# DeltaNet decays stacked at four partition offsets, two heads' state as one block-diagonal tile, and inverse products that alternate row groups

## The chip, the cores and the metric

The kernel runs on one NeuronCore of a Trainium2 chip. The metric is the device time of one execution in microseconds, from the first to the last instruction with what lies around them. Each kernel is run several times; the median counts.

## The reference, cut to what matters

The program is a network of two layers on 272 tokens (16 meta tokens and 256 of the input), width 1024. Each layer is an FFN, a mixer and another FFN. The mixer has four branches (two attentions, the gated DeltaNet and an RG-LRU); their outputs are gated and added. The DeltaNet branch, with `q`, `k` normalised and four heads of 64, works in chunks of 128 tokens:

```
g = -exp(a_log) * softplus(p_a + dt_bias);  beta = sigmoid(p_b)
G = cumsum(g) inside a chunk;  decay[i,j] = exp(G[i] - G[j]) for i >= j
m = I + strictly_lower(beta * (k k^T) * decay);   solve m for w, u
qk = lower((q k^T) * decay)
per chunk:  v_new = u - w S;  o = (q exp(G)) S + qk v_new
            S = S * exp(G_last) + (k exp(G_last - G))^T v_new
```

Everything is float32.

## The kernel before, in words

Activations stand transposed, features on partitions, tokens as columns. A product with a weight matrix is `wtile` (L437): a weight tile of 128x128 is split into a rounded part `wh` (ScalarE, L408) and a rest `wl` (VectorE, L410), and three fp32r matmuls add `wh`·`xh`, `wh`·`xl`, `wl`·`xh` into a PSUM tile `j` (`o`, `br`, `wo` in other places). These are called weight matmuls below. Weights come by DMA into `wf` and are split in pieces of 1024 columns, five pieces ahead at most.

The order on all engines is set when the program is built. Every branch is a Python generator (a chain); `poll` (L277) looks at each of them after a weight tile, and lets a chain issue its next step when a running estimate of the engines' clocks says that its input is there. Chain steps on TensorE are only looked at every third tile (`EVERY`), so nine weight matmuls stand between most of them. `mm` (L229) and `pe_go` (L211) hold the estimate of a matmul's cost; a tile of under 128 rows or columns is priced as if it ran alone. All engines take their instructions in the order so made.

The DeltaNet branch is two chains. `fab` (L1675) makes the decays. Twelve partitions, 96 to 107, hold the forget gate, the decay and beta of four heads; `gc` is the cumulated decay, `eg`, `be`, `eh` are exponentials. Twelve small transposes (L1731, tile `ns`), each of 12 partitions, bring four of these rows for three token tiles to token order, two selector products (`sel2`) add the last columns, and VectorE copies them to the SBUF tile `ns` and negates two parts of it. Then for each head a selector product on 12 partitions spreads `gc` over the rows (`dc`), three bf16 matmuls add the causal mask, one for each token tile, and ScalarE takes the exponential into `dec`. `nsv` (L1778) reads columns of `ns`.

`gdn` (L1878) and its helper chains do the rest. `g_qk` makes k·q (`kq`) and `gdn` k·k (`kk`), for each token tile and each half `e` of the partitions (two heads lie on partitions 0 to 63 and 64 to 127 of two tiles) two products into one PSUM tile. The matrix is then inverted in blocks of 16, by a VectorE loop of fifteen rounds (L1936), and combined to 32, 64 and 128 by products called p0, x0, p1, x1 (32x32 tiles, in four row groups of 32 partitions) and p2, x2 (64x64). In the profile their tiles are `p` and `x`. Last, for each token tile: k·S (`ks`) and q·S (`qs`), for each half two products of 64 rows into their own PSUM tile, `vn`, and the update `su` of the state `S`, which holds head pairs on two partition halves.

Of the kernel before, what the change touches and what calls it, by code (L numbers as in the profile page):

```python
# [71 lines left out]
class Prog:  # L72
# [471 lines left out]
    def setup2(self, c):  # L544
# [16 lines left out]
        self.maskk = self.const([P, P], BF16, "maskk")  # L561
# [14 lines left out]
        self.V(c, "tensor_copy", out=self.maskk, in_=mg)  # L576
# [5 lines left out]
        q = slice(96, 108)  # L582
# [3 lines left out]
        self.POOL(c, "affine_select", out=sel[q], in_=o4[q], pattern=[[-1, 4], [0, P]], compare_op=ALU.is_equal,  # L586
                                fill=0.0, base=-4, channel_multiplier=1)
# [17 lines left out]
        for x, dst in ((0, self.eye16), (1, self.st16)):  # L605
# [7 lines left out]
        self.POOL(c, "affine_select", out=misc[q, 512:768].rearrange("p (h c) -> p h c", h=4),  # L613
                                in_=self.ones[:, 0:1].to_broadcast([P, 256]).rearrange("p (h c) -> p h c", h=4)[q],
                                pattern=[[-1, 4], [0, 64]], compare_op=ALU.is_equal,
                                fill=0.0, base=-4, channel_multiplier=1)
# [1058 lines left out]
    def fab(self, c):  # L1675
# [26 lines left out]
        for a, n in TOK:  # L1702
            yield "dve"
            self.V(c, "tensor_tensor_scan", out=gc[q, a:a + n], data0=self.ones[q, 0:1].to_broadcast([12, n]), data1=lg[q, a:a + n],
                   initial=0.0, op0=ALU.mult, op1=ALU.add)
# [8 lines left out]
        eg, be = e, lg  # L1714
        for a, n in TOK:
            yield "dve"
            self.V(c, "tensor_scalar", out=eh[q, a:a + n], in0=gc[q, a:a + n], scalar1=gc[q, a + n - 1:a + n],
                   scalar2=-1.0, op0=ALU.subtract, op1=ALU.mult)
        yield AF.Exp
        self.A(c, eg[q, :T], gc[q, :T], AF.Exp)  # L1720
        yield AF.Exp
        self.A(c, be[q, :T], lg[q, :T], AF.Exp)
        yield AF.Exp
        self.A(c, eh[q, :T], eh[q, :T], AF.Exp)
        yield
        ps = yield from self.take_wait(c, "px", name="ns")
        for ti, (a, n) in enumerate(TOK):
            for x, src in enumerate((be, gc, eg, eh)):
                o = ti * 48 + x * 12
                yield "pe"  # L1730
                nc.tensor.transpose(ps[:n, o:o + 12], src[q, a:a + n], self.ident[q, 96:108])  # L1731
                self.pe_go(c, 13.0, 1, 107.0, 90.0)
        for pr in range(2):
            yield "pe"
            self.mm(c, ps[:, 160 + 3 * pr:163 + 3 * pr], self.sel2[q, pr, :],
                    eg[q, 15:T:128])
        yield
        ns = yield from self.take_wait(c, "S", name="ns")
        for ti, m in ((0, 16), (1, P), (2, P)):
            yield "dve"  # L1740
            self.V(c, "tensor_copy", out=ns[:m, ti * 48:ti * 48 + 48], in_=ps[:m, ti * 48:ti * 48 + 48])
        yield "dve"
        self.V(c, "tensor_copy", out=ns[:, 160:166], in_=ps[:, 160:166])
        self.give(ps, c.t)
        for ti, m in ((0, 16), (1, P), (2, P)):
            b = ti * 48

            yield "dve"
            self.V(c, "tensor_scalar", out=ns[:m, b:b + 4], in0=ns[:m, b + 8:b + 12], scalar1=-1.0, scalar2=None,
                   op0=ALU.mult)  # L1750
            yield "dve"
            self.V(c, "tensor_scalar", out=ns[:m, b + 12:b + 16], in0=ns[:m, b + 16:b + 20], scalar1=-1.0,
                   scalar2=None, op0=ALU.mult)
        self.ns = ns
        self.ev["ns"] = c.t
        yield

        dec = yield from self.take_wait(c, "L", [P, 4, T], name="dec")
        for h in range(4):
            ps = yield from self.take_wait(c, "px", name="dc")  # L1760
            yield "pe"
            self.mm(c, ps[:, :T], self.sel[q, h, :], gc[q, :T], True, False)
            for ti, (a, n) in enumerate(TOK):
                yield "pe"
                self.mm(c, ps[:, a:a + n], self.identb, self.maskk[:, :n], False, ti == 2)
            yield
            for ti, (a, n) in enumerate(TOK):
                yield AF.Exp
                self.A(c, dec[:n, h, a:a + n], ps[:n, a:a + n], AF.Exp,
                       bias=ns[:n, ti * 48 + 12 + h:ti * 48 + 13 + h])  # L1770
            self.give(ps, c.t)
            yield
        for s in st:
            self.give(s, c.t)
# [3 lines left out]
    def nsv(self, x, ti, n, h0=0, hs=4, step=1):  # L1778

        b = ti * 48 + (0, 12, 28, 40, 8)[x]  # L1780
        return self.ns[:n, b + h0:b + h0 + (hs - 1) * step + 1:step]
# [41 lines left out]
    def g_qk(self, c):  # L1823
# [4 lines left out]
        for ti in (1, 2, 0):  # L1828
            if ti == 0 and self.l == L - 1:
                continue  # L1830
            a, n = TOK[ti]
            for e in range(2):
                ps = yield from self.take_wait(c, "px", name="kq")
                p0 = 64 * e
                v = ps[:, 0:256].rearrange("p (x i) -> p x i", x=2)
                yield "pe"
                for x in range(2):
                    self.mm(c, v[:n, x, :n], self.cvt[f"gk{x}"][p0:p0 + 64, a:a + n],
                            self.cvt[f"gq{x}"][p0:p0 + 64, a:a + n])
                qd = QT[:, (ti - 1) * 4 + e:(ti - 1) * 4 + e + 3:2, :] if ti else self.mt[:, 4 + e:4 + e + 3:2, :]  # L1840
                yield "dve"
                self.V(c, "tensor_tensor", out=qd, in0=v[:n, :, :n], in1=self.dec[:n, e::2, a:a + n], op=ALU.mult)
                self.give(ps, c.t)
# [34 lines left out]
    def gdn(self, c):  # L1878
# [20 lines left out]
        for ti in (1, 2, 0):  # L1899
            a, n = TOK[ti]  # L1900
            for e in range(2):
                ps = yield from self.take_wait(c, "px", name="kk")
                p0 = 64 * e
                v = ps[:, 0:256].rearrange("p (x i) -> p x i", x=2)
                yield "pe"
# [3 lines left out]
                for x in range(2):  # L1909
                    h = e + 2 * x  # L1910
                    yield "dve"
                    self.V(c, "scalar_tensor_tensor", out=AT[:, (ti - 1) * 4 + h, :] if ti else mt[:, h, :],
                           in0=v[:n, x, :n], scalar=self.nsv(0, ti, n, h, 1),
                           in1=dec[:n, h, a:a + n], op0=ALU.mult, op1=ALU.mult)
                self.give(ps, c.t)
# [50 lines left out]
        for s in sl:  # L1966
            for hc in range(8):
# [7 lines left out]
        for s in sl:  # L1975
            for hc in range(8):
# [29 lines left out]
        for b in (0, 2):  # L2006
            for hc in range(8):
# [9 lines left out]
        for b in (0, 2):  # L2017
            s, t_ = sl[b], sl[b + 1]
            for hc in range(8):
                self.mm(c, v[s, hc, :], P1[t_, hc, :], Xh[t_, hc, :])  # L2020
                if b == 0:
                    self.mm(c, v[t_, hc, :], Xh[t_, hc, :], P1[t_, hc, :])
# [38 lines left out]
        outs = []  # L2061
        for ti in range(3):
# [3 lines left out]
            if ti:  # L2066
                for e in range(2):
                    ps = yield from self.take_wait(c, "px", name="ks")
                    p0 = 64 * e
                    v = ps[:, :P].rearrange("p (x d) -> p x d", x=2)  # L2070
                    yield "pe"
                    for x in range(2):
                        self.mm(c, v[:n, x, :], kn[x][p0:p0 + 64, a:a + n], S[p0:p0 + 64, x, :])
                    tk = yield from self.take_wait(c, "S", [P, 2, 64], name="tk")
                    yield "dve"
                    self.V(c, "tensor_tensor", out=tk[:n], in0=v[:n],
                           in1=self.nsv(2, ti, n, e, 2, 2)[:, :, None].to_broadcast([n, 2, 64]), op=ALU.mult)
                    self.give(ps, c.t)
                    yield "dve"
                    self.V(c, "tensor_tensor", out=h4(r[:n])[:, e::2, :], in0=h4(r[:n])[:, e::2, :], in1=tk[:n],  # L2080
                           op=ALU.subtract)
                    self.give(tk, c.t)
# [11 lines left out]
            if ti < 2:  # L2094
                S2 = yield from self.take_wait(c, "S", [P, 2, 64], name="S")
                ps = yield from self.take_wait(c, "px", name="su")
                yield "pe"
                for h in range(4):
                    p0 = 64 * (h % 2)
                    self.mm(c, ps[p0:p0 + 64, (h // 2) * 64:(h // 2) * 64 + 64], kd[:n, h * 64:(h + 1) * 64],  # L2100
                            r[:n, h * 64:(h + 1) * 64])
                for x in range(2):
                    yield "dve"
# [139 lines left out]
```

## Time and profile before

| | |
|---|---|
| median of three runs | 1363.91 us (1363.6 to 1367.29) |
| the profiled execution | 1363.22 us, span 1361.5 us |
| TensorE busy, instructions | 1338.8 us (98%), 10615 matmul records |
| VectorE busy | 879.6 us (65%) |
| ScalarE busy | 732.0 us (54%) |
| mean granted TensorE clock | 0.991 |

A float32 matmul shows as two records in the profile, a transpose and an fp32r matmul as one. The duration of a record has the way through the array in it, so records overlap; what a matmul costs the engine is read from the start of one to the start of the next.

### The profile page before, as it was taken

What the parts mean: (1) busy time and instruction counts of PE and PEld (TensorE: products, weight loads), DVE (VectorE), ACT (ScalarE), POOL (GpSimd) and SP (SyncE); (2) the same over time, 40 slices, a digit from 0 to 9 for tenths busy, and PEclk for the clock granted to TensorE, in tenths of its full rate; (3) what the DMA queues carried; (4) which work ended last, traced back from release to release, by engine and by line L of the source; (5) the groups of instructions that cost most, each with busy time, mean ns of one, the idle gap of its engine ahead of it and who ended that gap; (6) DMA issues with size and microseconds to landing.
All of it is one profiled execution on the core that took longest, in us unless ns stands there. A gap on an engine that the chain in (4) does not pass through costs nothing.

```text
span 1361.5 us, 25871 instructions
## 1 busy us (share of the span) xinstructions
PE 1338.8 (98%) x10615; PEld 1290.5 (95%) x10615; DVE 879.6 (65%) x1526; ACT 732.0 (54%) x1196; POOL 208.5 (15%) x287
## 2 busy tenths in 40 slices
PE   8999999999999999999999999999999999999997
PEld 7999999888999999999999999998889999999986
DVE  6765556668566876655566555567794678766653
ACT  5465445886454554444444445459843645644442
POOL 3533000000002242110011110010000032211100
PEclk9999999999799999999999999999998999999999
DMA  6666565332225555555555555653322365555551
GB/s 220 191 195 199 164 175 164 108 125 74 79 78 167 190 177 186 186 173 174 180 161 180 184 164 167 173 163 125 125 78 65 113 200 193 192 186 186 200 196 53
DMA packets 210886, 214.62 MB, mean 158 GB/s; under 512 B 13292, under 2 KB 200016, under 8 KB 210768
## 3 DMA queue, kind: packets, MB, share of 16 engines
q1 hardware_dynamic: 208608, 210.68, 48.1%
q0 software_dynamic: 2128, 2.29, 0.6%
q8 instruction: 83, 1.36, 0.4%
q14 instruction: 35, 0.29, 0.1%
q10 hardware_dynamic: 32, 0.01, 0.0%
HBM read 211.90 MB, written 1.05 MB: 156 GB/s over the span
## 4 chain that ended last, share of the span: by engine, by line
PE 81%; DVE 10%; ACT 6%; issue 2%; POOL 0%; DMA 0%; SPq 0%; ACTq 0%; DVEq 0%; POOLq 0%
PE j L230 52%; PE o L230 15%; PE fo L230 4%; DVE wl L183 3%; PE br L230 3%; ACT wh L207 2%; ACT L202 2%; PE wo L230 1%; PE x L230 1%; ACT gt L207 1%; DVE xl L183 1%; DVE sm L183 1%; PE p L230 1%; DVE tp L1939 1%; ACT sq L207 1%
## 5 line engine op out<-in xcount | busy, mean ns | idle before, releaser
L230 PE MATMUL j<-xh,wh 128*128 128x272 f32 (+2 forms) x2224 | 651.3, 293 | 0.1
L230 PE MATMUL j<-xh,wl 128*128 128x272 f32 (+2 forms) x2224 | 638.1, 287 | 0.1
L230 PE MATMUL j<-xl,wh 128*128 128x272 f32 (+2 forms) x2224 | 637.5, 287 | 0.0
L183 DVE TENSOR_TENSOR wl<-wf,wh 128x1024 fp32r<-128x1024 f32 (+2 forms) x406 | 492.3, 1221 | 176.0 <-ACT wh L207 175.1
L207 ACT ACTIVATE wh<-wf 128x1024 fp32r<-128x1024 f32 (+2 forms) x406 | 407.0, 1031 | 103.3 <-PE o L230 72.7
L230 PEld LDWEIGHTS j<-xh,wh 128*128 128x128 f32 (+1 forms) x2224 | 420.0, 189 | 4.6 <-issue 1.0
L230 PEld LDWEIGHTS j<-xl,wh 128*128 128x128 f32 (+1 forms) x2224 | 420.8, 189 | 0.6
L230 PEld LDWEIGHTS j<-xh,wl 128*128 128x128 f32 (+1 forms) x2224 | 420.6, 189 | 0.8 <-DVE wl L183 0.8
L230 PE MATMUL o<-act,wh 128*128 128x272 f32 x1056 | 198.9, 288 | 0.0
L230 PEld LDWEIGHTS o<-act,wh 128*128 128x128 f32 x1056 | 165.8, 188 | 0.0
L230 PE MATMUL o<-act,wl 128*128 128x272 f32 x528 | 152.1, 288 | 0.0
L194 POOL TENSOR_TENSOR g<-g,R 128x272 f32<-128x272 f32 (+1 forms) x88 | 86.4, 984 | 378.1 <-ACT g L207 378.1
L207 ACT ACTIVATE act<-g 128x272 fp32r<-128x272 f32 (+1 forms) x88 | 37.6, 428 | 135.2 <-DVE g L183 135.2
L207 ACT ACTIVATE g<-g 128x272 f32<-128x272 f32 (+1 forms) x88 | 37.4, 428 | 120.2 <-DVE g L183 119.7
L230 PEld LDWEIGHTS o<-act,wl 128*128 128x128 f32 x528 | 99.5, 188 | 0.0
L183 DVE TENSOR_TENSOR g<-j,g 128x272 f32<-128x272 f32 (+1 forms) x88 | 38.2, 434 | 54.6 <-PE j L230 51.1
L194 POOL TENSOR_TENSOR sq<-sq,sq 128x272 f32<-128x272 f32 (+1 forms) x36 | 32.8, 910 | 257.4 <-ACT sq L207 243.9
L202 ACT ACT_TABLE_LOAD x51 | 65.4, 1283 | 1.7 <-PEq L2231 0.8
L194 POOL TENSOR_TENSOR gt<-gt,gt 128x272 f32<-128x272 f32 (+1 forms) x32 | 35.4, 1130 | 198.1 <-DVE gt L183 198.0
L207 ACT ACTIVATE gt<-gt,pv 128x272 f32<-128x272 f32 (+1 forms) x64 | 30.0, 510 | 64.7 <-DVE gt L183 64.6
L183 DVE TENSOR_TENSOR g<-j,R 128x272 f32<-128x272 f32 (+1 forms) x88 | 37.9, 433 | 34.4 <-PE j L230 34.1
L230 PE MATMUL fo<-wh,act 128*128 128x512 f32 x176 | 55.3, 395 | 0.0
(332 smaller groups left out, 1377.8 us busy)
## 6 DMA issues: line engine op xcount, KB each, us to landing
wf<-in_ffn_wi_dram SPq DMA_DIRECT2D x86, 1024.0 KB, 5.2
wf<-in_ffn_wo_dram SPq DMA_DIRECT2D x34, 1024.0 KB, 5.2
wf<-in_w_gate_dram SPq DMA_DIRECT2D x32, 1024.0 KB, 5.2
wf<-in_w_in_dram SPq DMA_DIRECT2D x16, 1024.0 KB, 5.2
wf<-in_ffn_wo_dram SPq DMA_DIRECT2D x12, 768.0 KB, 4.8
wf<-in_w_branch_dram SPq DMA_DIRECT2D x16, 512.0 KB, 3.5
wf<-in_w_out_dram SPq DMA_DIRECT2D x8, 1024.0 KB, 5.4
wf<-in_w_in_dram SPq DMA_DIRECT2D x4, 512.0 KB, 3.9
```

What stands on the lines that cost most here:

```text
L183: getattr(self.nc.vector, op_)(**kw)
L194: getattr(self.nc.gpsimd, op_)(**kw)
L202: self.nc.scalar.preload_act_table_set(SETS[ok[0]])
L207: self.nc.scalar.activation(out=out, in_=in_, func=func, **kw)
L230: self.nc.tensor.matmul(out, lhsT, rhs, start=start, stop=stop)
L1939: nc.vector.stream_shuffle(tf[:, k * 12:], xf[:, k * 12:], mask=[k] * 16 + [16 + k] * 16)
```

## The change

In `fab` the rows that were in four tiles are written into one tile `pk`, zeroed before, at partitions 0 (beta), 32 (cumulated decay), 64 (its exponential) and 96 (decay to the end of the chunk). Three transposes of the whole tile replace the twelve. The selector products take all 128 partitions of `pk`. One mask of 272 columns takes the place of three mask matmuls for each head. k·q, k·k and the products p0, x0, p1, x1 are written so that neighbouring matmuls use different row groups; for k·q and k·k the two halves write two PSUM tiles. The state of two heads becomes a block-diagonal 128x128 tile, zeroed by GpSimd, so that k·S, q·S and the update are two products of 128 rows and columns each.

```diff
-        for _ in range(6):
+        for _ in range(5):
-        zs, e, sp, lg, gc, eh = st
+        zs, e, sp, lg, pk = st
+        nc.gpsimd.memset(pk[:, :T], 0.0)
+        g, u, w = slice(32, 44), slice(64, 76), slice(0, 12)
...
+        for ti, (a, n) in enumerate(TOK):
+            self.tr(c, ps[:n, ti * P:(ti + 1) * P], pk[:, a:a + n])
+        for pr in range(2):
+            self.mm(c, ps[:, 384 + 3 * pr:387 + 3 * pr], self.sel2[:, pr, :], pk[:, 15:T:128])
...
-        for ti, (a, n) in enumerate(TOK):
-            for x, src in enumerate((be, gc, eg, eh)):
-                o = ti * 48 + x * 12
-                yield "pe"
-                nc.tensor.transpose(ps[:n, o:o + 12], src[q, a:a + n], self.ident[q, 96:108])
...
-            self.mm(c, ps[:, :T], self.sel[q, h, :], gc[q, :T], True, False)
-            for ti, (a, n) in enumerate(TOK):
-                yield "pe"
-                self.mm(c, ps[:, a:a + n], self.identb, self.maskk[:, :n], False, ti == 2)
+            self.mm(c, ps[:, :T], self.sel[:, h, :], pk[:, :T], True, False)
+            self.mm(c, ps[:, :T], self.identb, self.maskk, False, True)
...
             for e in range(2):
-                ps = yield from self.take_wait(c, "px", name="kk")
-                p0 = 64 * e
-                v = ps[:, 0:256].rearrange("p (x i) -> p x i", x=2)
-                yield "pe"
-                for x in range(2):
-                    kk = kn[x][p0:p0 + 64, a:a + n]
-                    self.mm(c, v[:n, x, :n], kk, kk)
+                p2.append((yield from self.take_wait(c, "px", name="kk")))
+            v = [ps[:, 0:256].rearrange("p (x i) -> p x i", x=2) for ps in p2]
+            yield "pe"
+            for h in range(4):
+                kk = kn[h // 2][64 * (h % 2):64 * (h % 2) + 64, a:a + n]
+                self.mm(c, v[h % 2][:n, h // 2, :n], kk, kk)
...
-        for s in sl:
-            for hc in range(8):
+        for hc in range(8):
+            for s in sl:
                 self.mm(c, v[s, hc, :], AT[s, hc, s], Tc[s, hc, :])
...
+        for _ in range(2):
+            x = yield from self.take_wait(c, "S", [P, 2, P], name="S")
+            nc.gpsimd.memset(x.ap, 0.0)
+            states.append(x)
...
-                for e in range(2):
-                    ps = yield from self.take_wait(c, "px", name="ks")
...
-                    for x in range(2):
-                        self.mm(c, v[:n, x, :], kn[x][p0:p0 + 64, a:a + n], S[p0:p0 + 64, x, :])
+                ps = yield from self.take_wait(c, "px", name="ks")
+                yield "pe"
+                for x in range(2):
+                    self.mm(c, ps[:n, x * P:(x + 1) * P], kn[x][:, a:a + n], S[:, x, :])
```

The order on TensorE changes in these places.

TensorE in layer 0, where the decay columns are transposed (`ns`), before:

```order
L1731 MATMUL ns_2856<-ident_111,fab_2667 128x12
L230 MATMUL j_2928<-xh_82,wh_2769 128x272
L230 MATMUL j_2928<-xl_90,wh_2769 128x272
L230 MATMUL j_2928<-xh_82,wl_2770 128x272
L230 MATMUL j_2928<-xh_83,wh_2769 128x272
L230 MATMUL j_2928<-xl_91,wh_2769 128x272
L230 MATMUL j_2928<-xh_83,wl_2770 128x272
L230 MATMUL j_2928<-xh_84,wh_2797 128x272
L230 MATMUL j_2928<-xl_92,wh_2797 128x272
L230 MATMUL j_2928<-xh_84,wl_2798 128x272
L1731 MATMUL ns_2856<-ident_111,fab_2664 128x12
```

The same place in the changed kernel, behind the products and transposes of two attentions (`qu`, `vt`):

```order
L230 MATMUL qu_2812<-misc_2642,wq_1277 128x272
L241 MATMUL vt_2817<-ident_111,fv_372_2754 128x128
L241 MATMUL vt_2817<-ident_111,fv_377_2796 128x128
L241 MATMUL ns_2838<-ident_111,fab_2669 16x128
L241 MATMUL ns_2838<-ident_111,fab_2669 128x128 x2
L230 MATMUL ns_2838<-fab_2669,sel_778 128x3 x2
L230 MATMUL j_2798<-xh_83,wh_2707 128x272
```

The three transposes and the two selector products stand in one piece; the twelve single transposes, with nine weight matmuls between two of them, are gone.

TensorE in layer 0 at the k·q and k·k products (`kq`, `kk`; `cv` are q and k), before:

```order
L230 MATMUL j_3569<-xh_82,wl_3407 128x272
L230 MATMUL kq_3579<-cv_2987,cv_2894 128x128
L230 MATMUL kq_3579<-cv_3039,cv_2945 128x128
L230 MATMUL kk_3585<-cv_2894 128x128
L230 MATMUL kk_3585<-cv_2945 128x128
L230 MATMUL sc_3600<-ka_2562,qa_2561 128x144
```

And now:

```order
L230 MATMUL j_3375<-xh_85,wl_3249 128x272
L230 MATMUL kk_3389<-cv_2903 128x128
L230 MATMUL kk_3390<-cv_2903 128x128
L230 MATMUL kk_3389<-cv_2961 128x128
L230 MATMUL kk_3390<-cv_2961 128x128
L241 MATMUL nat_3415<-ident_111,cv_2903 128x128
```

The four products of a token tile go alternately into two PSUM tiles, and the group stands 63 weight matmuls earlier in the program, ahead of most of the attention scores (`sc`).

TensorE in layer 0 at the last steps of the inverse, p2 here, before:

```order
L230 MATMUL j_4365<-xh_82,wl_3978 128x272
L230 MATMUL sc_4351<-kt_2805,qt_2804 128x16
L230 LDWEIGHTS identb_698
L230 MATMUL sc_4351<-maskq_711,identb_698 128x16
L230 MATMUL pv_4406<-vl_2906,lt_4398 128x256
L230 MATMUL p_657_4412<-T_644_4307,AT_2573 64x64 x8
L241 MATMUL pl_4439<-ident_111,mp_4349 128x128
L241 MATMUL ot_4442<-ident_111,oa_4422 128x128 x2
L230 MATMUL j_4365<-xh_83,wh_3977 128x272
```

And now, where p2 is followed by five narrow score products with their masks (two shown) and x2 before the next weight matmul:

```order
L230 MATMUL p_650_4373<-T_633_4247,AT_2575 64x64 x8
L230 MATMUL sc_4381<-kt_2807,qt_2806 128x16
L230 LDWEIGHTS identb_698
L230 MATMUL sc_4381<-maskq_711,identb_698 128x16
L230 MATMUL sc_4366<-ka_2564,qa_2563 128x16
...
L230 MATMUL x_655_4403<-XF_4206,P_654_4394 64x64 x8
L230 MATMUL sc_4366<-ka_2564,qa_2563 128x16
L230 LDWEIGHTS identb_698
L230 MATMUL sc_4366<-maskq_711,identb_698 128x16
L241 MATMUL pl_4425<-ident_111,mp_4379 128x128
L230 MATMUL j_4270<-xh_86,wh_4007 128x272
```

Nine weight matmuls that stood between p2 and x2 now stand before p2.

## Rows read from the trace of the kernel before

**Rows 1.** The page, part 1: busy us, share, instructions of each engine.

```profile
PE 1338.8 (98%) x10615; PEld 1290.5 (95%) x10615; DVE 879.6 (65%) x1526; ACT 732.0 (54%) x1196; POOL 208.5 (15%) x287
```

**Rows 2.** The chain that ended last (start us, us, what), first FFN.

```profile
54.72 93.95 PE j L230 x750
```

**Rows 3.** Stretches: length; busy PE, PEld, DVE, ACT, POOL; granted clock; DMA share, GB/s.

```profile
360.58:374.23 13.65, 13.54 (x111) 12.46 (x109) 5.32 (x12) 6.92 (x28) 0.00 (x0) 0.50 0.24 78
1022.77:1029.60 6.83, 6.83 (x80) 5.95 (x79) 1.29 (x4) 1.90 (x6) 0.29 (x1) 0.50 0.01 2
...
301.40:348.20 46.80, 45.14 (x349) 40.97 (x349) 41.38 (x143) 30.63 (x75) 4.18 (x8) 1.00 0.25 80
976.90:1003.00 26.10, 24.03 (x198) 21.86 (x196) 23.91 (x81) 16.44 (x45) 0.70 (x2) 1.00 0.25 82
```

**Rows 4.** Timeline (start us, us, engine, line), layer 0, two decay transposes.

```profile
245.94 0.23 PE L1731 MATMUL ns<-ident,fab 12*128 12x12 f32 x1
...
247.41 0.23 PE L1731 MATMUL ns<-ident,fab 12*128 12x12 f32 x1
```

**Rows 5.** Timeline, layer 0: a product of two accumulated matmuls, a decay selector.

```profile
224.24 1.08 PE L230 MATMUL nq<-sq,ones 128*128 128x272 f32 x4
...
225.28 0.29 PE L230 MATMUL j<-xl,wh 128*128 128x272 f32 x1
...
259.62 0.28 PE L230 MATMUL j<-xh,wl 128*128 128x272 f32 x1
259.83 0.72 PE L230 MATMUL dc<-fab,sel 12*128 12x272 f32 x2
...
260.71 0.29 PE L230 MATMUL j<-xl,wh 128*128 128x272 f32 x1
```

**Rows 6.** Timeline, layer 0: k·q and k·k, mixed and alone.

```profile
307.28 0.27 PE L230 MATMUL kk<-cv 64*128 64x128 f32 x1
307.29 0.27 PE L230 MATMUL kq<-cv,cv 64*128 64x128 f32 x1
307.39 0.27 PE L230 MATMUL kk<-cv 64*128 64x128 f32 x1
...
309.72 0.71 PE L230 MATMUL kk<-cv 64*128 64x128 f32 x4
310.36 0.39 PE L230 MATMUL j<-xh,wh 128*128 128x272 f32 x1
```

**Rows 7.** Timeline, layer 0: one k·S group between weight matmuls.

```profile
380.99 0.29 PE L230 MATMUL br<-yh,wl 128*128 128x272 f32 x1
381.21 0.66 PE L230 MATMUL ks<-S,cv 64*128 64x64 f32 x4
381.79 0.39 PE L230 MATMUL br<-yh,wh 128*128 128x272 f32 x1
382.02 0.28 PE L230 MATMUL br<-yl,wh 128*128 128x272 f32 x1
```

**Rows 8.** Timeline, layer 1: p0, x0, and x1 in pairs.

```profile
1020.73 1.91 PE L230 MATMUL p<-Tc,AT 32*32 32x32 f32 x64 [0.18 <-DVE Tc L1959]
...
1023.72 3.06 PE L230 MATMUL x<-Xh,P 32*32 32x32 f32 x64
...
1034.90 0.21 PE L230 MATMUL x<-Xh,P 32*32 32x32 f32 x1
1034.91 0.21 PE L230 MATMUL x<-P,Xh 32*32 32x32 f32 x1
...
1035.30 0.19 PE L230 MATMUL x<-Xh,P 32*32 32x32 f32 x1
```

**Rows 9.** The chain that ended last, layer 0, at half clock.

```profile
371.91 2.04 PE j L230 x9
```

**Rows 10.** TensorE's wait for the inverse; the page's group of ScalarE table loads.

```profile
PE p L230 <- DVE Tc L1959: 0.7, 2, 0.5
...
L202 ACT ACT_TABLE_LOAD x51 | 65.4, 1283 | 1.7 <-PEq L2231 0.8
```

More of the change, by code (lines that the diff above doesn't have):

```diff
@@ L560, in setup2 @@
         self.maskq = self.const([P, P], BF16, "maskq")
[L561 removed]
+        self.maskk = self.const([P, T], BF16, "maskk")
         yield "pool"
@@ L575, in setup2 @@
         yield "dve"
-        self.V(c, "tensor_copy", out=self.maskk, in_=mg)
+        self.V(c, "tensor_copy", out=self.maskk[:, 0:NM], in_=mg[:, 0:NM])
+        for b in range(2):
+            yield "dve"
+            self.V(c, "tensor_copy", out=self.maskk[:, NM + b * P:NM + (b + 1) * P], in_=mg)
         st = self.const([P, P], F32, "st")
@@ L1703, in fab @@
             yield "dve"
-            self.V(c, "tensor_tensor_scan", out=gc[q, a:a + n], data0=self.ones[q, 0:1].to_broadcast([12, n]), data1=lg[q, a:a + n],
-                   initial=0.0, op0=ALU.mult, op1=ALU.add)
+            self.V(c, "tensor_tensor_scan", out=pk[g, a:a + n], data0=self.ones[q, 0:1].to_broadcast([12, n]),
+                   data1=lg[q, a:a + n], initial=0.0, op0=ALU.mult, op1=ALU.add)
+        yield AF.Exp
+        self.A(c, pk[u, :T], pk[g, :T], AF.Exp)
+        yield AF.Exp
+        self.A(c, pk[w, :T], lg[q, :T], AF.Exp)
+        for a, n in TOK:
+            yield "dve"
+            self.V(c, "tensor_scalar", out=e[g, a:a + n], in0=pk[g, a:a + n], scalar1=pk[g, a + n - 1:a + n],
+                   scalar2=-1.0, op0=ALU.subtract, op1=ALU.mult)
+        yield AF.Exp
+        self.A(c, pk[q, :T], e[g, :T], AF.Exp)
+        ps = yield from self.take_wait(c, "px", name="ns")
+        yield "pe"
[3 more added lines that the diff above has]
+            self.mm(c, ps[:, 384 + 3 * pr:387 + 3 * pr], self.sel2[:, pr, :], pk[:, 15:T:128])
+        ns = yield from self.take_wait(c, "S", name="ns")
+        for t0, k, m in ((1, 2, P), (0, 1, 16)):
+            src = ps[:m, t0 * P:(t0 + k) * P].rearrange("p (x c) -> p x c", c=32)
+            dst = ns[:m, t0 * 64:(t0 + k) * 64].rearrange("p (x c) -> p x c", c=16)
+            yield "dve"
+            self.V(c, "tensor_copy", out=dst[:, :, 4:12], in_=src[:, :, 4:12])
+            for x, o in ((0, 8), (1, 4)):
+                yield "dve"
+                self.V(c, "tensor_scalar", out=dst[:, x::4, 0:4], in0=src[:, x::4, o:o + 4], scalar1=-1.0,
+                       scalar2=None, op0=ALU.mult)
+        yield "dve"
+        self.V(c, "tensor_copy", out=ns[:, 192:198], in_=ps[:, 384:390])
+        self.give(ps, c.t)
+        self.ns = ns
+        self.ev["ns"] = c.t
         yield "dve"
@@ L1974, in gdn @@
         yield "pe"
-        for s in sl:
-            for hc in range(8):
+        for hc in range(8):
+            for s in sl:
                 self.mm(c, v[s, hc, :], P1[s, hc, :], Xh[s, hc, :])
@@ L2005, in gdn @@
         yield "pe"
-        for b in (0, 2):
-            for hc in range(8):
+        for hc in range(8):
+            for b in (0, 2):
                 self.mm(c, v[sl[b + 1], hc, :], AT[sl[b], hc, sl[b + 1]], Tc[sl[b], hc, :])
@@ L2016, in gdn @@
         yield "pe"
[L2017 to L2022, printed above, removed]
+        for hc in range(8):
+            for o, t_, x, y in ((sl[0], sl[1], P1, Xh), (sl[2], sl[3], P1, Xh), (sl[1], sl[1], Xh, P1)):
+                self.mm(c, v[o, hc, :], x[t_, hc, :], y[t_, hc, :])
         while not sd.done:
@@ L2128, in gdn_out @@
         if ti:
[L2129 to L2139 removed]
+            ps = yield from self.take_wait(c, "px", name="qs")
+            yield "pe"
+            for x in range(2):
+                self.mm(c, ps[:n, x * P:(x + 1) * P], self.cvt[f"gq{x}"][:, a:a + n], S[:, x, :])
+            yield "dve"
+            self.V(c, "tensor_tensor", out=h4(oq[:n]), in0=h4(ps[:n, 0:256]),
+                   in1=self.nsv(2, ti, n)[:, :, None].to_broadcast([n, 4, 64]), op=ALU.mult)
+            self.give(ps, c.t)
         ps = yield from self.take_wait(c, "px", name="o")
```

148 lines of the change are left out of this document (50 added, 98 removed).

## The prediction

> **What bounds the kernel now.** I read the page first: TensorE is busy 98% of the span, VectorE 65%, ScalarE 54% [rows 1]. A busy TensorE is a hint only, so I then read start times in the timeline: in the FFN 750 weight matmuls of 272 columns take 93.95 us [rows 2], 0.125 us each, nine in 1.13 us. The change touches no FFN work. Inside the mixer (215 to 405 us for layer 0, 901 to 1077 us for layer 1) the same weight matmuls go on, with the small matmuls of the four branches put between them. TensorE works in order, so whatever a small matmul adds between two weight matmuls is added to the end, unless something else is waited for there. That is the case in two stretches, 301 to 348 and 977 to 1003 us, where VectorE is busy 41.4 of 46.8 and 23.9 of 26.1 us [rows 3]: there VectorE is nearly as full as TensorE. And in two stretches the granted clock is half, 13.65 us in layer 0 and 6.83 us in layer 1 [rows 3], each begun right after 32x32 matmuls of the inverse. So the terms are: TensorE time of the removed or packed small matmuls, the low clock, and what VectorE and ScalarE won't let through.
>
> **The change part by part.** The sum is made against the profiled execution, 1363.2 us (span 1361.5), 0.7 below the median of 1363.9. All per-layer terms count twice.
>
> *Decay columns.* Before, twelve transposes of 12 partitions per layer stand one by one between rounds of nine weight matmuls. From one to the next is 247.41 - 245.94 = 1.47 us [rows 4]; nine weight matmuls alone are 1.13, so each costs 0.34, and twelve 4.1 us. After, there are three of 128 columns in a row. The nearest rows for a 128-column step are starts 0.11 apart [rows 6], so 0.3 us. The two selector products stay. Saved: 3.8 per layer, **7.5** in all (6.5 to 8).
>
> *Decay matrices.* A selector product on 12 partitions: from the weight matmul before it (259.62) to the second one behind (260.71) 1.09 us, less two at 0.125 makes 0.84. Two products of the same width on all 128 partitions: 225.28 - 224.24 = 1.04, less the one between makes 0.91, or 0.46 each [rows 5]. Four per layer at 0.38 less: 1.5, **3.0** in all. Three bf16 mask matmuls become one as wide as the three; taken as nothing (0 to 1 per layer gained).
>
> *Products k·q and k·k.* A group of two products (four records) takes 0.64 us, 309.72 to 310.36. Where the old order happened to put a k·q group of one row half beside a k·k group of the other, they ran in pairs: k·k at 307.28, k·q at 307.29, the next k·k at 307.39, so two records in 0.11 [rows 6]. The new code issues every group so. Two groups, 1.28 us, become 4 x 0.11 plus the fixed 0.2 that the four leave of 0.64, so 0.64. Eight such pairs of groups make 5.1; less 0.7 for those that were paired already, plus 0.6 for the narrow ones: **5.0** in all.
>
> *State products.* k·S: 380.99 to 382.02, 1.03 less 0.25 makes 0.78 [rows 7], eight per layer with q·S, half of them next to other small work, where the four records have 0.58 (381.21 to 381.79): 5.5 us. After: four, each of four 128-column records, 4 x 0.11 plus 0.1 for what the next weight matmul starts late: 2.1. Saved 3.4 per layer, **6.8** in all. The update of S keeps its time (eight records of 64 columns become four of 128): 0, within 0.4 either way.
>
> *32x32 products of the inverse.* Sixty-four records take 1.91 us, 1.72 without the tail, 0.027 each [rows 8]; per layer p0 and x0 have 64, p1 has 32 (half of that, 0.86), x1 48 (16 pairs, priced below, and sixteen alone: 0.9): 5.2 us. The only rows that show overlap between such tiles are x1, where two tiles in one row group go in pairs 0.033 us apart at most (twelve pairs from 1034.90 to 1035.30, later ones 0.03), or 0.015 a record [rows 8]. No row shows four row groups at once. By 0.015 the new time is 160 x 0.015 + 16 x 0.03 = 2.9, saved 2.3 per layer, **4.6** in all. Bounds: nothing at all, or 3.5 per layer if all four run at once (0.43 for each of the four steps). I take the x1 rows since they are the same shape.
>
> A rule speaks against this term. In the old pairs k·q and k·k write two different PSUM tiles; p0, x0 and p1 put their row groups into one PSUM tile. The Trainium skill, "TensorEngine Tiling (Array Packing)", Restrictions and Gotchas, says that different row tiles can't access the same PSUM bank at once. By that rule this term would be 0 and the other packed ones (k·q, k·k, which now get a PSUM tile for each row half) untouched; no row here shows row groups in one tile, so the trace can't settle it, and it is a rival below.
>
> *Clock.* At the low clock a round of nine weight matmuls takes 2.04 instead of 1.13, and 64 records of x0 take 3.06 where p0 took 1.91 [rows 8, 9]: 38 to 45% is lost, about 0.42 of 20.5 us, 8.6 us at most. In layer 1 the engine fell to 1.2 GHz right behind p0 (1020.73 + 1.91 against 1022.77), in layer 0 behind p0, x0 and p1. These get shorter, and in layer 1 the new order puts value products of the attention between p0 and x0. In layer 0 the new order puts p2, ten narrow score matmuls and x2 in one piece without a weight matmul, which looks like what ran before the fall. I take layer 1's stretch as gone and layer 0's as halved: 2.9 + 2.9 = **5.8** (0 to 8.6).
>
> *What is not let through.* The k·q and k·k products stand at the head of the stretches where VectorE is full, and the new order only moves the loop of the inverse a few weight pieces earlier, so I count their 5.0 as lost. ScalarE gets two more table loads (51 become 53) of 1.28 us [rows 10]; one is counted. Lost: **6.3** (0 to 12). The rest costs nothing: VectorE has twelve instructions less, the POOL memsets (one of 272 columns before the scans, two of 256 before the state loop, per layer) are issued long before their readers while POOL is idle 85% of the time [rows 1]; in front of the scans the memset is a new wait on VectorE, with weight splits queued behind it, but six ScalarE and VectorE steps lie between its issue and the first scan. Wider constants are made behind the first FFN.
>
> Sum: 7.5 + 3.0 + 5.0 + 6.8 + 4.6 = 26.9, plus 5.8, less 6.3: 26.4 us. 1363.2 - 26.4 = 1336.8, and with 0.7 for the median **1337 us**.
>
> **The rivals.**
> Packing doesn't pack: 32x32 row groups that write one PSUM tile go one after the other, at the 0.027 a record of p0 before. 1337 + 4.6 = 1342. For it: no row shows the contrary. Against it: x1 shows two outputs in one tile at once.
> The clock falls as it does now, since small matmuls still stand together: 1337 + 5.8 = 1343.
> VectorE and ScalarE are the bound of the mixer after all: only the decay terms, which lie where TensorE is full, come through (10.5), and some 3 of the state products: 1350. For it: the 41.4 of 46.8 us. Against it: VectorE is free for a third of the span [rows 1], and the new order spreads the loop's work ahead.
> Slower than before: the planner still prices 32x32 and 64-row matmuls as if they ran singly, so TensorE arrives early at each step of the inverse and state chain (13 steps a layer: p0 to x2, three products for v, two k·S, two updates) and stands there, weight matmuls queued behind. It waited 0.7 us in two such places [rows 10]. To be slower by 0.3% the 26 steps would have to wait 30.5 us more, 1.2 each; at 1.3 us each the time is 1371. Nothing in the trace shows a wait of that size on these steps, and between most steps stand nine weight matmuls, 1.13 us.
> No change: the same mechanism at about 1 us a step, or 26 us lost in VectorE.
>
> **How the numbers follow.** Forecast as summed 0.42, packing fails 0.13, clock stays 0.16, VectorE bound 0.15, no change 0.07, slower 0.07. A difference under 0.3% (4 us) can't be told from none here. Faster: 0.42 + 0.13 + 0.16 + 0.15 = 0.86; same 0.07; slower 0.07. The range reaches down to four tiles at once (2.4 more), the clock never falling (2.8) and nothing lost (6.3), 1326, and up past the VectorE rival, to 1354.
>
> **What would show it.** Right: nine weight matmuls and then no transposes between them; k·k records in pairs 0.11 us apart; p0 in about 1 us; k·S in four records; mixers shorter by some 13 us each, FFN unchanged; half clock in at most 10 us before the end. Wrong: p0 still at 0.027 a record (no packing); half clock for 20 us or more; idle time of TensorE ahead of p, x, vn or weight matmuls grown from the present few us to 20 (planner or VectorE).

## The result and the profile after

The changed kernel takes 1344.18 us (median of four runs, 1341.55 to 1348.35) where the kernel before took 1363.76: ratio 0.9855, 95% interval 0.9843 to 0.9867, 19.6 us less by the medians. The profiled execution is the fastest of the four, 1341.55 us with a span of 1339.8. The four runs differ mainly by TensorE's clock: 1341.55 at a mean granted clock of 0.996, 1343.60 at 0.995, 1344.77 at 0.994, 1348.35 at 0.990.

The page's first part, columns as in [rows 1]:

```profile
PE 1309.3 (98%) x10533; PEld 1270.9 (95%) x10533; DVE 877.0 (65%) x1514; ACT 732.8 (55%) x1198; POOL 209.8 (16%) x293
```

The shares are those of before; TensorE is busy 29.5 us less, which says little about where, since overlapping records count once. So first the length of each layer's part, from the start of the tile `o` of an FFN to the start of the mixer's output product `wo`. In layer 1 that takes in the two FFNs between the mixers, which the change doesn't touch. Stretches of the kernel before, columns as in [rows 3]:

```profile
148.50:474.10 325.60, 321.56 (x2611) 305.57 (x2610) 219.53 (x457) 191.36 (x354) 32.55 (x48) 0.98 0.42 132
...
631.70:1142.40 510.70, 506.46 (x4145) 490.21 (x4144) 330.19 (x590) 277.44 (x456) 55.56 (x74) 0.99 0.48 152
```

The same stretches of the changed kernel:

```profile
149.30:461.20 311.90, 304.69 (x2570) 293.32 (x2569) 217.79 (x450) 188.54 (x352) 32.77 (x51) 0.99 0.44 137
...
619.60:1121.20 501.60, 492.64 (x4103) 481.86 (x4102) 328.75 (x583) 281.25 (x460) 56.92 (x77) 1.00 0.48 155
```

Layer 0's part is 13.7 us shorter, layer 1's 9.1. Length less busy PE is the time in which TensorE stood: 4.04 + 4.24 us before, 7.21 + 8.96 after. The half clock before is in [rows 3]; after, it is two stretches (the last 4 to 6 us of every kernel, which are at half clock too, are left out here and below):

```profile
363.78:367.19 3.41, 3.41 (x19) 2.63 (x17) 0.94 (x3) 3.39 (x10) 0.00 (x0) 0.50 0.00 0
1056.68:1060.10 3.42, 3.42 (x19) 3.42 (x18) 2.74 (x4) 1.83 (x2) 0.00 (x0) 0.50 0.03 9
```

From here on each part's length is split in three: waits (as above), half clock (half of the time that ran at it, lost) and work (the rest, what the matmuls cost at full clock, from start to start). For both layers together the change took work from 817.7 to 793.9 us (-23.8), half clock from 10.2 to 3.4 (-6.8) and waits from 8.3 to 16.2 (+7.9): -22.7. Half of the time is a little too much for what the low clock costs: nine weight matmuls took 2.04 us at it instead of 1.13, which is 45%, and by the prediction's 0.42 the clock gave 5.7 and work 24.9. Outside these parts it is 1.0 us longer (the first `o` starts at 149.3 instead of 148.5), so the profiled execution is 21.7 us shorter.

Now the edits one by one, from the timeline of the changed kernel (start us, us, engine). Decay columns and decay matrices in layer 0, for [rows 4, 5]:

```profile
239.50 0.49 PE L241 MATMUL ns<-ident,fab 128*16 128x128 f32 x3
239.83 0.51 PE L230 MATMUL ns<-fab,sel 128*128 128x3 f32 x4
240.20 0.37 PE L230 MATMUL j<-xh,wh 128*128 128x272 f32 x1
...
242.55 0.62 PE L230 MATMUL dc<-fab,sel 128*128 128x272 f32 x2
243.01 0.28 PE L230 MATMUL dc<-maskk,identb 128*128 128x272 bf16 x1
```

Three transposes take 0.33 us (239.50 to 239.83), and a selector product 0.46 (242.55 to 243.01): both as worked out. k·k in layer 0, for [rows 6], and k·S, for [rows 7]:

```profile
284.48 0.72 PE L230 MATMUL kk<-cv 64*128 64x128 f32 x8
285.15 0.66 PE L241 MATMUL nat<-ident,cv 128*128 128x128 f32 x4
285.57 0.37 PE L230 MATMUL j<-xh,wh 128*128 128x272 f32 x1
...
371.15 0.61 PE L230 MATMUL ks<-S,cv 128*128 128x128 f32 x4
371.52 0.37 PE L230 MATMUL br<-yh,wh 128*128 128x272 f32 x1
```

Eight k·k records go in 0.67 us, where four of one row half took 0.64; k·S takes 0.37. The inverse in layer 1, for [rows 8]: p0, p1 and a moment of x1.

```profile
1010.29 0.75 PE L230 MATMUL p<-Tc,AT 32*32 32x32 f32 x64
1010.97 0.70 PE L230 MATMUL pv<-vl,lt 128*128 128x256 f32 x2
...
1015.88 0.69 PE L230 MATMUL p<-Tc,AT 32*32 32x32 f32 x32
1016.50 0.39 PE L230 MATMUL j<-xh,wh 128*128 128x256 f32 x1
...
1019.32 0.21 PE L230 MATMUL x<-Xh,P 32*32 32x32 f32 x1 [1.22 <-ACT P L207]
```

p0's 64 records take 0.68 us from their start to the next matmul, 0.011 each instead of 0.029; p1's 32 over two row groups 0.62, 0.019 each. x1 stands 1.22 us for ScalarE's copy of P: TensorE is there before it. Such waits are new. TensorE's waits in layer 0's part (what waits, for whom, us in total, times, longest), which answer [rows 10], and the two longest of layer 1's:

```profile
PE sc L230 <- DVE QT L183: 1.6, 2, 1.3
PE x L230 <- issue: 1.0, 1, 1.0
PE nat L241 <- ACT r L207: 1.0, 1, 1.0
PE ku L230 <- ACT lt L207: 1.0, 1, 1.0
PE pt L241 <- ACT pr L207: 0.8, 1, 0.8
...
PE br L230 <- DVE gt L183: 2.3, 1, 2.3
PE ot L241 <- DVE oa L183: 1.4, 2, 0.8
```

Two of the first five stand right behind steps that became cheaper: `nat` behind `kq`, `ku` behind `kk`. `sc` waits for what VectorE makes of `kq`, with nine weight matmuls right before it. The wait of `x` is a stop of 1.05 us before the last record of x0, for which the profile shows no releaser.

### The profile page after: what moved, and what is told of

It reads as the page before. It is cut to its first block, busy times and chain, and to the rows that moved or that the text cites. A ratio compares the mean times of both kernels' runs of the same rounds, so it can differ in the third digit from the quotient of the medians.

```text
span 1339.8 us, 25708 instructions
## 1 busy us (share of the span) xinstructions
PE 1309.3 (98%) x10533; PEld 1270.9 (95%) x10533; DVE 877.0 (65%) x1514; ACT 732.8 (55%) x1198; POOL 209.8 (16%) x293
## 3 DMA queue, kind: packets, MB, share of 16 engines
HBM read 211.90 MB, written 1.05 MB: 159 GB/s over the span
## 4 chain that ended last, share of the span: by engine, by line
PE 79%; DVE 9%; ACT 8%; issue 2%; POOL 0%; DMA 0%; SPq 0%; ACTq 0%; DVEq 0%; POOLq 0%
PE j L230 51%; PE o L230 15%; PE fo L230 5%; PE br L230 3%; DVE wl L183 3%; ACT wh L207 3%; ACT L202 2%; PE wo L230 1%; PE pv L230 1%; ACT sq L207 1%; DVE xl L183 1%; ACT cv L207 1%; DVE cv L183 1%; ACT gt L207 0%; PE sc L230 0%
```

## The experiments

All times are medians beside runs of the kernel before on the same chip. Work, half clock and waits are those of the two parts together, from each kernel's profiled execution.

| kernel | median us | ratio to before (95%) | work | half clock | waits |
|---|---|---|---|---|---|
| before | 1363.8 to 1364.5 | 1 | 817.7 | 10.2 | 8.3 |
| changed | 1344.2 | 0.9855 (0.9843 to 0.9867) | 793.9 | 3.4 | 16.2 |
| inverse alone | 1358.2 | 0.9954 (0.9939 to 0.9969) | 812.4 | 6.8 | 11.1 |
| changed, inverse undone | 1347.7 | 0.9883 (0.9860 to 0.9906) | 799.7 | 5.1 | 13.9 |
| decays alone | 1352.4 | 0.9912 (0.9897 to 0.9927) | 810.1 | 5.1 | 9.5 |
| state alone | 1359.5 | 0.9964 (0.9954 to 0.9974) | 811.2 | 10.2 | 9.9 |
| k·q, k·k alone | 1359.6 | 0.9962 (0.9949 to 0.9975) | 815.3 | 3.4 | 12.4 |
| before, prices mended | 1360.4 | 0.9973 (0.9963 to 0.9983) | 822.3 | 3.4 | 6.7 |
| changed, prices mended | 1330.7 | 0.9752 (0.9736 to 0.9769) | 792.0 | 1.7 | 8.2 |
| changed, inverse's price mended | 1335.5 | 0.9790 (0.9776 to 0.9805) | 792.9 | 1.7 | 11.5 |
| changed, k·q and k·k price mended | 1331.8 | 0.9762 (0.9746 to 0.9779) | 792.4 | 3.4 | 8.9 |
| changed, prices more wrong | 1343.5 | 0.9848 (0.9833 to 0.9862) | 794.2 | 3.4 | 16.2 |

**The inverse alone, and undone.** In both only the order inside four bursts differs, so they measure the alternation by itself.

```diff
-        for s in sl:
-            for hc in range(8):
+        for hc in range(8):
+            for s in sl:
                 self.mm(c, v[s, hc, :], AT[s, hc, s], Tc[s, hc, :])
```

> The kernel before with one edit: the records of p0, x0, p1 and x1 are written so that neighbouring ones use different row groups. Nothing else on any engine moves, word for word the same order. In the trace of the changed kernel p and x cost 1.40 + 1.15 us less in layer 0 and 1.55 + 0.90 in layer 1, 5.0 in all, and x1 waited 1.2 us for ScalarE's copy of P. Theory (the alternation packs, the clock falls because of these long small steps): p0 at 0.011 us a record, 5 us less matmul time, some 1 to 2 us given back in waits of x1 and the steps behind, the 20.5 us at half clock of layers 0 and 1 cut to about 7, which is 5.7 us: 1363.8 - 9 = 1354 to 1356. Rival 1 (packing, but the clock falls for other reasons): half clock stays near 20 us, 1359 to 1361. Rival 2 (the 0.011 comes from where the step stands in the new order, not from the alternation): 1363 to 1364 and p0 at 0.029.

Measured 6.3 us less. p0 in layer 0 of this kernel (the record's length, and its wait), and p0 in the changed kernel with the alternation undone:

```profile
351.24 0.75 PE L230 MATMUL p<-Tc,AT 32*32 32x32 f32 x64 [0.53 <-DVE Tc L1959]
```

```profile
337.88 1.91 PE L230 MATMUL p<-Tc,AT 32*32 32x32 f32 x64
```

Rival 2 falls: the alternation does it, wherever the step stands. Work is down 5.3, waits up 2.8. Half clock fell from 20.5 to 13.7 us, between theory and rival 1, and so did the time.

> The changed kernel with that one edit undone: p0, x0, p1 and x1 row group after row group, as before; all else in the same order. Theory: p and x cost 5.0 us more, the waits of x0 (1.0) and x1 (1.2) fall away, half clock before the end rises from the 7 to 17 us that the four runs of the changed kernel show by their mean clock to about 20, 1.5 to 5 us: 1344.2 + 5.0 - 2 + 3 = 1350 (1347 to 1352). Rival 1 (clock not from these steps): 1347. Rival 2 (alternation does nothing): 1344.

3.8 us more by the ratios, at the lower end of the theory's range, which rival 1 shares: work 5.8 more, waits 2.3 less, half clock in the parts 1.7 more. Both kernels agree that the alternation is worth 5 to 6 us of work, of which 2 to 3 come back as waits. Whether these bursts bring the half clock on is not settled by them: in the kernel undone layer 1 had none.

**What one record costs.** The first four loops of the burst kernel, written in short, with `k` a PSUM tile, `s` a row group and `i` a block of columns:

```
p_row:   for s: for i:  mm(k0[s, i], A[s, i], B[s, i])
p_alt:   for i: for s:  mm(k0[s, i], A[s, i], B[s, i])
p_alt4:  for i: for s:  mm(k[s][s, i], A[s, i], B[s, i])
p_col4:  for i: for s:  mm(k[s][0:32, i], A[s, i], B[s, i])
```

> Not the network: bursts of fp32 products of 128 tokens of the input on TensorE, 80 or more full products ahead and eight between two bursts, so that what one record costs is read by start times; the output holds one of these products and not the reference. Bursts: 32 products of 32x32 row group after row group into one PSUM tile (as before), the same alternating over four row groups into one PSUM tile (as now), alternating into four PSUM tiles, alternating over four row groups that all write partitions 0 to 31 of four PSUM tiles, two row groups alternating; four products of 64 rows by 128 columns of one row half, and of both halves alternating into two PSUM tiles; two full products of 128 columns; four of 64 rows and 64 columns. Theory (what counts is that neighbours use other row groups and other partitions of the output, one PSUM tile or four is the same): 0.029, 0.011, 0.011, then 0.011 to 0.029, 0.019 us a record. Rival (row groups that write one PSUM tile still hinder each other): four tiles 0.007 to 0.008, one tile 0.011. Halves: 0.11 us a record alone and 0.055 alternating; full 0.11.

The first two bursts in the third round, between rows of full products (`wm`), and from the first round the start of the burst into four PSUM tiles, what follows it, and the burst of two row groups:

```profile
131.83 0.38 PE L29 MATMUL wm<-B,A 128*128 128x256 f32 x1
132.13 1.91 PE L29 MATMUL ka<-B,A 32*32 32x32 f32 x64
133.97 3.72 PE L29 MATMUL wm<-B,A 128*128 128x256 f32 x16
137.62 0.75 PE L29 MATMUL ka<-B,A 32*32 32x32 f32 x64
138.31 3.72 PE L29 MATMUL wm<-B,A 128*128 128x256 f32 x16
```

```profile
61.06 0.21 PE L29 MATMUL ka<-B,A 32*32 32x32 f32 x1
...
61.74 3.72 PE L29 MATMUL wm<-B,A 128*128 128x256 f32 x16
...
69.72 1.20 PE L29 MATMUL ka<-B,A 32*32 32x32 f32 x64
70.86 3.72 PE L29 MATMUL wm<-B,A 128*128 128x256 f32 x16
```

From first start to the next `wm`: 1.837 us row group after row group, 0.682 alternating into one PSUM tile, 0.683 into four tiles, 0.683 into four tiles on the same partitions 0 to 31, 1.130 for two row groups; the same in all three rounds within 0.001. Per record 0.0287, 0.0107, 0.0107, 0.0107, 0.0177. The theory holds and the rival falls: one PSUM tile or four makes no difference. Halves of 64 rows: eight records 1.085 alone and 0.645 alternating, 0.136 and 0.081 with the change of shape in them, 40% less rather than half. Two full products 0.444, four of 64 rows and columns 0.599.

**Each other part alone.** The hunks of the diff on the decays, the state and the k·q and k·k groups are put into the kernel before one at a time; a line or two of each is shown again. Costs by tile here and below are from the start of a record to the next start, waits taken out.

```diff
+        for ti, (a, n) in enumerate(TOK):
+            self.tr(c, ps[:n, ti * P:(ti + 1) * P], pk[:, a:a + n])
```

> The kernel before with the stacked decays alone (one tile at four partition offsets, three transposes, selector products on 128 partitions, one mask product a head); k·q, k·k, inverse and state as before. The planner orders anew what comes behind. Theory (the prediction's terms 7.5 and 3.0 stand, nothing is late behind them): 1364 - 10.5 = 1353.5 (1352 to 1356). Rival 1 (the terms are smaller, since some of the twelve transposes already stood beside other small work and the wide ones cost 0.7 a layer; by the trace of the changed kernel ns and dc themselves lose 5.4 in all and the weight matmuls behind them 2.2): 1356 to 1357. Rival 2 (given back in waits or half clock): 1360 to 1364.

12.2 us less, the theory's time, but by luck and not by its sum: work is down 7.6, not 10.5, waits up 1.2, and 5.1 came from half clock. By tiles `ns` lost 3.2, `dc` 2.2 and the weight matmuls 2.9, while the new order made `kq` and `kk` 1.4 dearer.

```diff
-                        self.mm(c, v[:n, x, :], kn[x][p0:p0 + 64, a:a + n], S[p0:p0 + 64, x, :])
+                    self.mm(c, ps[:n, x * P:(x + 1) * P], kn[x][:, a:a + n], S[:, x, :])
```

> The kernel before with the block-diagonal state alone (two products of 128 rows and columns for each k·S, q·S and update, two tiles zeroed by GpSimd). Theory (prediction): 6.8 less, 1357 (1356 to 1358.5). Rival (the trace of the changed kernel: ks and qs lose 6.0, su gains 0.6, and the chain of the state behind them waits more, since TensorE comes sooner): 3 to 5 less, 1359 to 1361.

5.0 less, the rival's time: work down 6.5, waits up 1.6, half clock as before.

```diff
-                    self.mm(c, v[:n, x, :n], kk, kk)
+                self.mm(c, v[h % 2][:n, h // 2, :n], kk, kk)
```

> The kernel before with k·q and k·k alternating between the two row halves and two PSUM tiles, and nothing else. Prediction: 5.0 of matmul time saved, and all of it lost again where VectorE is nearly as full as TensorE: 1364 within 1.5, with some 5 us more waits of TensorE between 300 and 350 and between 975 and 1005 us. Rival (the saving comes through): 1359. Rival (by the trace of the changed kernel k·q and k·k lose 2.4 in all, not 5.0): 1361 to 1362, waits unchanged.

5.0 less, the time of the rival in which the saving comes through, and again for another reason. Half clock fell by 6.8; work by 2.4 only (`kq` 1.5 and `kk` 1.2), and 4.1 of waits came on top. Most of these waits are one stop for which the profile shows no releaser, neither VectorE nor another:

```profile
PE pl L241 <- issue: 3.3, 1, 3.3
```

That the part brings nothing fell; whether VectorE takes back what TensorE saves is tested next.

**The planner's prices.** The planner prices a small matmul as alone. This edit gives it what the traces show, in ns for one record:

```diff
+    PACKED = {(32, 32): 13.0, (64, 64): 67.0, (64, 128): 66.0}
...
-        if tile != (128, 128):
+        if tile in self.PACKED:
+            one = self.PACKED[tile]
+        elif tile != (128, 128):
             one += load
```

> The changed kernel, only the planner's price of small matmuls is another: 13 ns for each of the two records of a 32x32 product, 67 for 64x64, 66 for 64 rows by 128 columns, as the trace of the changed kernel shows them, in place of 61, 117 and 220. Every order behind the first mixer step is planned anew. TensorE's waits in the two mixers are 7.2 and 9.0 us in the trace of the changed kernel, 4.0 and 4.2 before. Theory (the waits grew because the planner thinks TensorE later than it is, and lets it arrive early at x0, x1, pt, sc): waits back to about 8 us for both layers, 1344 - 8 = 1336. Rival (they grew because VectorE and ScalarE are full in these stretches): the waits stay near 16 us, 1344 within 3.

1330.7 us, 1.0% under the changed kernel and 2.5% under the kernel before: the fastest version of this study. Waits fell from 16.2 to 8.2, where they were before the change, work by 1.9 and half clock by 1.7. So of the 13.5 us between the medians some 10 are waits and work; the rest is clock, 1.7 here and more in the other runs (a mean clock of 0.990 to 0.996 before this edit, 0.996 in all four behind it).

The same in the kernel before, with the prices of its own trace:

```diff
+    PACKED = {(32, 32): 29.0, (64, 64): 67.0, (64, 128): 110.0}
```

> The kernel before, only the planner's price of small matmuls is another: for each of two records 29 ns for 32x32, 67 for 64x64, 110 for 64 rows by 128 columns, as its own trace shows them, in place of 61, 117 and 220. In the changed kernel the prices of its own trace gave 1344.2 to 1330.7. Theory (the wrong prices hurt the changed kernel because its packed products are further from them: its waits were 16.2 us in both mixers against 8.3 before): before gains little, 1360 to 1364, waits near 8 us. Rival (the planner was as wrong for both, and the better order has nothing to do with the change): 1350 to 1354.

4.1 less, as the theory says: waits hardly move (8.3 to 6.7), work grows by 4.6, and most of the gain is half clock. The wrong prices cost the changed kernel some 14 us, and the kernel before 4. Between the two kernels with mended prices lie 29.7 us; their work differs by 30.3.

The changed kernel with one of the prices mended at a time:

```diff
-    PACKED = {(32, 32): 13.0, (64, 64): 67.0, (64, 128): 66.0}
+    PACKED = {(32, 32): 13.0, (64, 64): 67.0}
```

> The changed kernel with the planner's price corrected only for the inverse (13 ns a record for 32x32, 67 for 64x64); k·q and k·k keep 220. With both corrected it was 1330.7 instead of 1344.2. Theory (each wrong price pulls TensorE ahead of the plan from its step on; the 104 products of 32x32 a layer are priced some 10 us too long, the k·q and k·k products some 4): two thirds of the 13.5 us come with the inverse alone, 1335 (1333 to 1338). Rival 1 (the head counts, since the waits in front of sc, ku, nat and kk stand ahead of the inverse): 1340 to 1343. Rival 2 (any new order of the planner moves the time by several us, and the corrected one was lucky): anywhere, 1328 to 1350.

As the theory says, 1335.5. But the waits fell in layer 1 alone (from 8.96 to 4.46). In layer 0 they stay at 7.04 (7.21 in the changed kernel), with those at the head of the chain as they were (line numbers are three higher here, by the edit):

```profile
PE sc L233 <- DVE QT L184: 1.5, 2, 1.2
PE nat L244 <- ACT r L208: 1.0, 1, 1.0
PE ku L233 <- ACT lt L208: 1.0, 1, 1.0
```

The next one shows that the parts don't add:

```diff
-    PACKED = {(32, 32): 13.0, (64, 64): 67.0, (64, 128): 66.0}
+    PACKED = {(64, 128): 66.0}
```

> The changed kernel with the price corrected only for products of 64 rows by 128 columns (66 ns a record in place of 220); the inverse keeps its old prices. Theory: 4 to 5 us of the 13.5, 1340 (1338 to 1342), the waits of x stay. Rival 1 (the head counts): 1332 to 1336. Rival 2 (luck of the order): anywhere.

1331.8, at the lower edge of rival 1. The price at the head of the chain alone gives nearly all, and brings the waits from 16.2 to 8.9; in layer 0 they are 3.46, and those of `sc`, `nat`, `ku` and x0 are gone. Its timeline at the first k·k and k·q groups in layer 0, to be put beside the changed kernel's rows at 284.48 above:

```profile
285.25 0.72 PE L233 MATMUL kk<-cv 64*128 64x128 f32 x8
285.89 0.39 PE L233 MATMUL j<-xh,wh 128*128 128x272 f32 x1
...
287.12 0.60 PE L244 MATMUL nat<-ident,cv 128*128 128x128 f32 x4
...
289.24 0.71 PE L233 MATMUL kq<-cv,cv 64*128 64x128 f32 x8
289.89 0.39 PE L233 MATMUL j<-xh,wh 128*128 128x272 f32 x1
...
291.39 0.66 PE L244 MATMUL nat<-ident,cv 128*128 128x128 f32 x4
```

And k·q in the changed kernel:

```profile
286.88 0.72 PE L230 MATMUL kq<-cv,cv 64*128 64x128 f32 x8
288.63 0.55 PE L241 MATMUL nat<-ident,cv 128*128 128x128 f32 x3 [1.04 <-ACT r L207]
```

The changed kernel issues the transposes `nat` directly behind k·k and k·q, since by the old price eight records have filled 1.76 us, more than nine weight matmuls; they take 0.67. With the price mended nine weight matmuls stand between, and the wait of the second `nat` (1.04 us) falls to 0.1. Two stretches of this kernel, 300 to 340 us:

```profile
300.00:320.00 20.00, 19.15 (x164) 17.93 (x163) 18.89 (x72) 15.42 (x37) 2.17 (x2) 1.00 0.24 81
320.00:340.00 20.00, 19.89 (x148) 18.24 (x148) 19.14 (x65) 12.85 (x35) 1.48 (x3) 1.00 0.33 106
```

And the same in the changed kernel:

```profile
300.00:320.00 20.00, 18.73 (x153) 17.60 (x152) 19.12 (x77) 12.85 (x34) 1.20 (x1) 1.00 0.25 79
320.00:340.00 20.00, 19.04 (x255) 17.05 (x253) 17.00 (x48) 11.41 (x30) 1.02 (x1) 1.00 0.33 108
```

VectorE is fuller with the mended price (38.0 of 40 us against 36.1), and TensorE stands less (1.0 against 2.2). A full VectorE did not hold TensorE up here; the order did. One of the new waits stays: that of `br` in layer 1, 2.3 us in the changed kernel, is 2.1 here and with both prices mended (with the inverse's alone it is gone).

Last, the prices made more wrong:

```diff
-    PACKED = {(32, 32): 13.0, (64, 64): 67.0, (64, 128): 66.0}
+    PACKED = {(32, 32): 92.0, (64, 64): 176.0, (64, 128): 330.0}
```

> The changed kernel with the same prices made still more wrong: 92 ns a record for 32x32, 176 for 64x64, 330 for 64 rows by 128 columns, 1.5 times what the planner has. Theory (too high prices cost time in waits): more waits than the 16.2 us of both mixers, 1350 (1346 to 1356). Rival 2 (luck of the order): as likely below 1344 as above.

1343.5, waits 16.2 as with the old prices: the theory's 1350 fell, and rival 2 fits. Why more error costs no more is not shown; a step that already stands directly behind another can't come earlier. Luck of the order is not excluded by so few orders, but the three with a mended price lie at 1330.7 to 1335.5 and the two with wrong ones at 1343.5 and 1344.2, and the rows at `nat` show the mechanism at one place.

## Why the prediction was right

The time, 1344.2, lies in the range (1326 to 1354) and on the forecast side; it is 7 us above 1337. Step by step, in us saved over both layers:

| step | predicted | shown by tile | work, part alone |
|---|---|---|---|
| decay columns | 7.5 | 6.1 (`ns` 3.2, weight matmuls 2.9; alone) | 7.6 with the next |
| decay matrices | 3.0 | 2.2 | |
| k·q and k·k | 5.0 | 2.1 (2.9 with mended prices, 2.7 alone) | 2.4 |
| state | 6.8 | 5.5 (`ks` 3.2, `qs` 2.9, `su` 0.6 dearer) | 6.5 |
| 32x32 products | 4.6 | 5.0, 5.4 alone | 5.3 |
| sum of these | 26.9 | 20.9, with small products that moved 23.8 | 21.8 |
| clock | 5.8 | 6.8 (5.7 at 0.42) | |
| given back | -6.3 | -7.9 | |

**Sizes on the after side were right; k·q, k·k and the decays were too large on the before side.** New transposes (0.3 predicted, 0.33 shown), the selector product (0.46, 0.46), a pair of k·k groups (0.64, 0.67) and k·S (0.53 with the late start of the next matmul, 0.46) came about as worked out. But the prediction took what a group costs from places where it stands alone and multiplied it by the number of groups. The wide k·q and k·k groups would have cost 10.2 us so, or 9.5 with the 0.7 it took off for pairs; all their records in the trace of before cost 7.5, since 48 of the 64 stood in mixed stretches, more than [rows 6] suggested. Of the 24 decay transposes 5 stood beside other work than weight matmuls, which explains a part of that miss. The step that failed is the multiplication: adding up every record by tile was possible in the trace of before. For the state it held, 6.5 of work against 6.8 (the 5.5 by tile leaves out what the weight matmuls beside it start late), for there the prediction had half of the groups next to other small work. The update `su`, taken as nothing within 0.4 a layer, cost 0.3 a layer. The 32x32 products were priced too low before, 0.027 a record, with the length of the last one taken off, against the 0.0287 that the burst kernel shows to the start of the next matmul.

**The packing rival fell.** The price of 0.015 a record, from pairs in one row group [rows 8], was too cautious: 0.011 with all four row groups. The Trainium skill, "TensorEngine Tiling (Array Packing)", Restrictions and Gotchas, says that different row tiles can't access one PSUM bank at once. For row groups that write different partitions of one PSUM tile (512 float32 columns) the measurement shows no hindrance: 0.682 us against 0.683 with four tiles. Row groups that write the same partitions of one tile were not tried.

**The clock came out in sum, not in place.** Half clock went from 20.5 to 6.8 us before the end. That is the 13.7 us less that were forecast, and partly luck: layer 1 was predicted to have none and layer 0 half, but each has 3.4. Over the changed kernel's runs 0.990 against 0.996 of mean clock is 16 us more at half clock (0.006 x 1345 x 2) and 6.8 us more time, 0.42 for each, the prediction's factor. This is also why the median lies 2.6 above the profiled execution, where 0.7 was allowed. The parts tried alone add to 15.3 of half clock, more than the 10.2 there was: that part of a gain can be had once. With it their medians (12.2 + 5.0 + 5.0 + 6.3 = 28.5) come to more than the whole change brought.

**The loss came near in size by luck, for its cause was another.** The prediction lost 5.0 to a full VectorE and 1.3 to ScalarE's table loads (53 now, as it said). The waits did grow by 7.9 and stand in part where it put them, at the head of the chain, but mended prices take them back to 8.2 while VectorE is fuller. The rival "slower" had the mechanism, a planner that lets TensorE arrive early, and was priced at 1.2 us on each of 26 steps. The waits of about a microsecond that it needs do stand there, but at a handful of places; the other steps still have weight matmuls in front.

So the profiled execution missed 1336.8 by 4.7: 3.1 in work, 1.6 in waits, 1.0 outside the parts, less 1.0 that the clock gave more (at 0.42: 2.0 in work, and nothing from the clock).

## What to carry to other kernels

Where a planner places work by a price for each instruction, an edit that makes instructions cheaper must change the prices too: here that was worth 13.5 us on top of 20, some 10 of it in waits and work, while the same in the kernel before gave 4, most of it clock. Size a saving by adding every record that will change, not by one isolated place times a count. Small products in different rows of the array should alternate row groups; their outputs may lie on different partitions of one PSUM tile, or in several.

## What the runs showed of the hardware

Four row groups of 32x32 fp32 products overlap to 0.0107 us a record from 0.0287, two to 0.0177, and it made no difference whether four groups wrote their own partitions of one PSUM tile or the same partitions of four. In the burst kernel the last full product before a burst of small ones took 0.309 us to the next start, before one of full ones 0.216: the change of shape cost 0.09. Half clock fell at other places in kernels whose order differs only inside four bursts, and in six of the kernels once in the first FFN as well; what brings it on stays open.
